# Low parts of the weight chunks by accumulating transfers issued from GpSimd, in place of a VectorE subtraction

## The chip, the core and the metric

One core of a Trainium2 chip runs the kernel. The metric is the device time of one execution in microseconds. The kernel before takes 1121.04 us (median of 2 runs, 1120.94 to 1121.14). Engines are named as in the profile: PE (TensorE; PEld is its weight load), DVE (VectorE), ACT (ScalarE), POOL (GpSimd), SP (SyncE, which issues the transfers here).

## The reference

Two transformer-like blocks run one after the other on x of 512 tokens by 1024 features, all in float32. Cut to the parts that give the large matrix products:

```python
def first_block(x, mem, ...):
    proj = rmsnorm(x, norm_g) @ w_in                  # 1024 x 4616
    y_a = mlstm_branch(...) * silu(z_a)
    y_b = pool_branch(...) * silu(z_b)
    y_c = mem_attn_branch(qc, mem, ..., w_mem_kv) * silu(z_c)
    return rmsnorm(x + concat([y_a, y_b, y_c]) @ w_out, final_norm_g)

def second_block(h, ...):
    p = h @ w_in_2 + b_in_2                           # 1024 x 7184
    y_a = spatial_gating(a_u, a_v, ...)
    y_b = gla_chunked(q, k, v, log_f) * ... * silu(r)
    h = layer_norm(ALPHA * h + (sigmoid(g_a) * y_a + sigmoid(g_b) * y_b) @ w_out_2)
    return layer_norm(ALPHA * h + square(relu(h @ w_ff1)) @ w_ff2)
```

## The kernel before, in words

**Products in parts.** Each float32 operand is split in a high part (rounded to the fp32r type of the PE) and a low part (the operand less its high part). A product is then three matmuls: high by high, high by low, low by high (`mm3`).

**Chunks.** The weights lie in HBM as 184 chunks of 128 partitions by 1024 (18 of them by 1040) float32, in the order of use; all are 512 KB, or 520 KB. `load_to` (line 631) has SP transfer chunk c to a tile `wr` (4 buffers). `split_to` (line 639) makes the high part `wh` on ACT (a Copy that rounds) and the low part `wl` on DVE (`wr` less `wh`); both have 4 buffers (`HL`, line 612). One chunk is the weights of one unit on PE, most often 8 x 3 matmuls of 512 columns (`fm`, line 718) or 16 x 3 of 256 or 260 columns (`units_tok`, line 812). `run_ahead` (line 698) names the chunks to be split while a unit runs.

**Which chunks go another way.** Chunks 0 and 1 are split piece by piece at the start (low parts on POOL). The 22 chunks 124 to 145 (`fast_ff`) go through `pair_weights` (line 731), which splits sums of them. Chunks 117 to 123 and 160 to 183 are `paged`: split into pages `pg`, in two halves. The rest (2 to 116, 146 to 159) goes through the line that the change touches, line 655.

**Order.** The program is recorded first (`Recorder`), each operation with a cost (`costs`, line 225). `schedule` (line 360) then runs a model of the engines and the buffers and writes the order of each engine's queue; transfers share one modelled wire there. Each engine works through its queue in that order, and waits in it. The order is the same in every execution.

**Side work.** Between the units the branches run in small steps: the mlstm heads and the attention early, the gated linear attention (`gla`, line 1593) in the middle, with many small POOL additions, then the layer norms. POOL also makes the residual (`resid`, line 1855).

The line at the heart of it and the helper that it calls:

```python
def split(hi, lo, src, scale=None, eng=None):
    if scale is None:
        act(hi, src, ACTF.Copy)
        tt(eng or V, lo, src, f(hi), ALU.subtract)
```

Of the kernel before, what the change touches and what calls it, by code (L numbers as in the profile page):

```python
# [11 lines left out]
ACTF = mybir.ActivationFunctionType  # L12
ALU = mybir.AluOpType
# [7 lines left out]
ISQ = 128.0 ** -0.5  # L21

SLOT = 1088

NFAST = 11

# [143 lines left out]
class Recorder:  # L170
# [54 lines left out]
    def costs(self, o):  # L225

        kw, eng = o.kw, o.eng
        out = kw["out"]
        n = out.n if isinstance(out, View) else 512
        ins = [v for k, v in kw.items() if isinstance(v, View) and k not in WRITES]  # L230
        ps = any(v.tile.psum for v in ins)
        o.port, o.table, o.tail = False, None, 60
        if eng == "PE":
            o.tail = 230
            if o.what == "transpose":
                o.cost = 112
            else:
                n = kw["rhs"].n
                slow = kw["rhs"].dt == F32
                o.cost = 2 * max(112, 0.85 * n) if slow else max(113, 0.449 * n)  # L240
        elif eng == "ACT":
            extra = sum(isinstance(kw.get(k), View) for k in ("scale", "bias"))
            o.cost = (150 if ps else 190) + 0.835 * n + 95 * extra + (206 if "accum_out" in kw else 0)
            fn = kw["func"].name if hasattr(kw["func"], "name") else str(kw["func"]).rsplit(".", 1)[-1]
            o.table = EXACT.get(fn)
        elif eng == "DVE":
            n = max(n, max((v.n for v in ins), default=0))
            ptr = any(isinstance(kw.get(k), View) for k in ("scalar", "scalar1", "scalar2"))
            big = [k for k in ("in_", "in0", "in1", "data", "mask", "data0", "data1") if isinstance(kw.get(k), View)]
            sb = [k for k in big if not kw[k].tile.psum]  # L250
            o.port = len(sb) >= 2 or (len(sb) == 1 and len(big) == 1 and o.what in ("tensor_copy", "tensor_scalar"))
            o.cost = 140 + 1.045 * n + 65 * ptr
            if o.what == "memset":
                o.cost = 50 + n
            elif o.what == "tensor_scalar" and not ps and n >= 256:
                o.cost = 140 + 0.55 * n + 65 * ptr
            elif o.what == "copy_predicated":
                o.cost = 160 + 1.1 * n
            elif o.what == "tensor_tensor_scan":
                o.cost = 1200  # L260
            elif n <= 16:
                o.cost = 165
        elif eng == "POOL":
            o.port = o.what != "memset"
            o.cost = 190 + 2.15 * n
            if o.what == "memset":
                o.cost = 515
            elif o.what == "affine_select":
                o.cost = 260 + 0.75 * n
            elif o.what == "tensor_copy":  # L270
                o.cost = 200 + 1.3 * n
        else:
            o.cost = 440
            o.tail = 2100
# [85 lines left out]
    def schedule(self, caps, prio):  # L360
        import heapq
        import numpy as np
        ops = self.ops
        n = len(ops)
        tags = list(caps)
        live = {g: np.zeros(n + 1, np.int32) for g in tags}
        for t in {t for o in ops for t in o.tiles}:
            t.left = 0
            if t.tag:
                live[t.tag][t.first] += 1  # L370
                live[t.tag][t.last + 1] -= 1
        for g in tags:
            live[g] = np.cumsum(live[g])
            assert live[g].max() <= caps[g], (g, live[g].max())
        for o in ops:
            for t in o.tiles:
                t.left += 1
        slots = {g: [0.0] * caps[g] for g in tags}
        ends = {}
        engines = ("PE", "ACT", "DVE", "POOL", "SP")  # L380
        at = dict.fromkeys(engines, 0.0)
        pend = {e: [] for e in engines}
        for o in ops:
            o.waiting, o.ready, o.start = len(o.deps), 0.0, None
        for o in ops:
            if not o.waiting:
                insort(pend[o.eng], (prio[o.i], o.i))
        head = 0
        port = 0.0
        wire = 0.0  # L390
        table = None
        best = {}
        fits = {}

        made = set()

        def room(o):

            need = {}
            for t in o.tiles:  # L400
                g = t.tag
                if not g or t in made:
                    continue
                need[g] = need.get(g, 0) + 1
                if len(slots[g]) < need[g]:
                    return False
                if t.first > head and live[g][head:t.first].max() >= caps[g]:
                    return False
            return True

        def look(e):
            got = None
            k = 0
            for _, i in pend[e]:
                o = ops[i]
                if not room(o):
                    continue
                s = max(at[e], o.ready)
                for t in o.tiles:
                    if t.tag and t not in made:  # L420
                        s = max(s, slots[t.tag][0])
                if o.port:
                    s = max(s, port)
                if got is None or s < got[0] - 1e-6:
                    got = (s, i)
                if s <= at[e] + 1e-6:
                    break
                k += 1
                if k > 60:
                    break  # L430
            return got

        done = 0
        order = []
        while done < n:
            for e in engines:
                best[e] = look(e) if pend[e] else None
            have = [(b[0], b[1], e) for e, b in best.items() if b]
            assert have, ("stuck", head, ops[head].eng, ops[head].what, {e: len(p) for e, p in pend.items()}, {g: len(s) for g, s in slots.items()})
            s, i, e = min(have)  # L440
            o = ops[i]
            pend[e].remove((prio[i], i))
            cost = o.cost
            if o.table and table not in o.table:
                table = o.table[0]
                cost += 1283
            if e == "SP":
                b = o.kw["out"]
                size = 4.0 * 128 * (b.n if isinstance(b, View) else 512)
                wire = max(wire, s + 500) + size / 250.0  # L450
                o.end = max(wire, s + cost) + 1500
            else:
                o.end = s + cost + o.tail
            o.start = s
            at[e] = s + cost
            if o.port:
                port = s + cost
            for t in o.tiles:
                if t.tag and t not in made:
                    heapq.heappop(slots[t.tag])  # L460
                    if t.first > head:
                        live[t.tag][head:t.first] += 1
                made.add(t)
            for t in o.tiles:
                t.left -= 1
                ends[t] = max(ends.get(t, 0.0), o.end)
                if not t.left and t.tag:
                    heapq.heappush(slots[t.tag], ends.pop(t))
                    if t.last >= head:
                        live[t.tag][head:t.last + 1] -= 1  # L470
            for j in o.users:
                u = ops[j]
                u.ready = max(u.ready, o.end if u.eng != e else s + cost + (0 if e != "SP" else o.end - s - cost))
                u.waiting -= 1
                if not u.waiting:
                    insort(pend[u.eng], (prio[j], j))
            while head < n and ops[head].start is not None:
                head += 1
            order.append(i)
            done += 1  # L480
        self.end = max(o.end for o in ops)
        return order
# [32 lines left out]
def tile_two_blocks(ctx, tc, wa, wb, xT, memT, vec, cst, rows, poolw, wst, wg2, out):  # L515
# [41 lines left out]
    def act(out, in_, func, **kw):  # L557
        A.activation(out=out, in_=in_, func=func, **kw)
# [44 lines left out]
    src = []  # L603
    na = nb = 0
    for kind in chunks:
# [3 lines left out]
        else:  # L609
            src.append(wb[nb])  # L610
            nb += 1
    RAW, HL = 4, 4
    raw, wsp, paged = {}, {}, set()
    FF1 = 4 + len(ORDER1) + 12 + 16 + len(ORDER2) + 8
    fast_ff = set(range(FF1 + 4, FF1 + 4 + 2 * NFAST))
# [23 lines left out]
    def split_to(i):  # L639
        while n_sp[0] <= min(i, NCH - 1):  # L640
            c = n_sp[0]
# [9 lines left out]
            else:  # L651
                o = shift.get(c, 0)
                h = rec.tile(sb, [128, SLOT], F32R, tag="wh", name=f"wh{c}", bufs=HL)[:, o:o + n]
                l = rec.tile(sb, [128, SLOT], F32R, tag="wl", name=f"wl{c}", bufs=HL)[:, o:o + n]
                split(h, l, t)
            wsp[c] = (h, l)
            n_sp[0] += 1

# [1659 lines left out]
```

## Time and profile before

| | before |
|---|---|
| median of 2 runs | 1121.04 us |
| the profiled execution, its own time | 1119.03 us |
| span of the profiled execution | 1117.3 us |
| PE busy | 1100.6 us (99%) |
| DVE busy | 771.1 us (69%) |
| ACT busy | 564.2 us (50%) |
| POOL busy | 182.7 us (16%) |
| transfers: bytes, share of 16 engines | 108.94 MB, 30.1% (queue q1) |
| mean granted clock of PE | 0.996 |

Busy times are sums over instructions of one profiled execution. The span goes from its first to its last instruction; its own time is 1.7 us more than the span. Issuing a transfer is not counted as busy. All recorded operations have one source line in the profile (L502), so groups are told apart by their tiles.

### The profile page before, as it was taken

The page shows a single profiled execution, that of the slowest core. Times are in us where ns is not written, and L with a number is a line of the kernel's source. Part 1 is how long each engine was busy: PE and PEld are TensorE (multiplying, and loading weights), DVE is VectorE, ACT ScalarE, POOL GpSimd, SP SyncE. Part 2 cuts the span into 40 slices and gives each one's busy share as a digit, 9 for nine tenths or more (in the row PEclk, how much of TensorE's full clock was granted, in tenths as well). Part 3 has the DMA queues.
Part 4 walks back from the last instruction along what each step waited for, and adds up shares of the span by engine and source line. Part 5 has one row for each costly group of instructions (what it writes and reads, how often), then busy time and mean ns, then how long its engine had stood idle before and what let it go on. Part 6 is the DMA issues. An engine that isn't in the chain of part 4 may idle for free.

```text
span 1117.3 us, 16271 instructions
## 1 busy us (share of the span) xinstructions
PE 1100.6 (99%) x6204; PEld 958.1 (86%) x6204; DVE 771.1 (69%) x1411; ACT 564.2 (50%) x964; POOL 182.7 (16%) x244
## 2 busy tenths in 40 slices
PE   7999999999999999999999999999999999999996
PEld 7888888878889999888888887899999988888885
DVE  6978888887336566667868876988898966233324
ACT  7766536444225343874655544446866666123301
POOL 5202101000012000253237550001000000000005
PEclk9999999999999999999999999999999999999998
DMA  8334322433322322232211132240133353244201
GB/s 303 114 104 148 108 76 67 151 101 108 95 94 92 101 76 76 78 94 85 84 57 57 57 98 72 89 139 1 61 111 114 114 171 96 91 132 133 75 1 76
DMA packets 33806, 108.94 MB, mean 98 GB/s; under 512 B 3888, under 2 KB 5040, under 8 KB 33728
## 3 DMA queue, kind: packets, MB, share of 16 engines
q1 hardware_dynamic: 33728, 107.90, 30.1%
q8 instruction: 49, 0.80, 0.3%
q14 instruction: 29, 0.24, 0.1%
HBM read 105.79 MB, written 2.10 MB: 97 GB/s over the span
## 4 chain that ended last, share of the span: by engine, by line
PE 96%; ACT 2%; DVE 1%; DMA 0%; issue 0%; SPq 0%; DVEq 0%
PE ps L502 96%; ACT pg L502 1%; DVE pg L502 1%; DVE wl L502 0%; DMA pg<-in_xT_dram 0%; ACT wh L502 0%; DVE sm L502 0%; SPq L502 0%; DVE sel L502 0%; DVE selc L502 0%; DVEq L502 0%
## 5 line engine op out<-in xcount | busy, mean ns | idle before, releaser
L502 PE MATMUL ps<-pg,wh 128*128 128x512 f32 (+1 forms) x1600 | 485.7, 386 | 0.0
L502 PEld LDWEIGHTS ps<-pg,wh 128*128 128x128 f32 x1600 | 294.4, 188 | 59.4 <-PE ps L502 0.7
L502 PE MATMUL ps<-pg,wl 128*128 128x512 f32 (+1 forms) x800 | 305.9, 383 | 0.0
L502 ACT ACTIVATE wh<-wr 128x1024 fp32r<-128x1024 f32 (+2 forms) x137 | 139.8, 1021 | 241.1 <-PE ps L502 209.0
L502 PE MATMUL ps<-pg,pg 128*128 128x512 f32 (+3 forms) x1264 | 236.5, 343 | 0.1
L502 ACT ACTIVATE pg<-pg 128x512 f32<-128x512 f32 (+7 forms) x328 | 174.2, 554 | 110.7 <-DVE pg L502 100.3
L502 PEld LDWEIGHTS ps<-pg,pg 128*128 128x128 f32 x1264 | 203.8, 191 | 28.8 <-ACT pg L502 0.6
L502 DVE TENSOR_TENSOR wl<-wr,wh 128x1024 fp32r<-128x1024 f32 (+1 forms) x129 | 165.0, 1282 | 76.8 <-ACT wh L502 76.3
L502 POOL TENSOR_TENSOR pg<-pg,pg 128x128 f32<-128x128 f32 (+4 forms) x113 | 109.3, 975 | 646.1 <-ACT pg L502 467.9
L502 PEld LDWEIGHTS ps<-pg,wl 128*128 128x128 f32 x800 | 150.2, 188 | 29.9
L502 PE MATMUL ps<-wh,pg 128*128 128x260 f32 (+2 forms) x800 | 168.1, 306 | 5.7 <-ACT wh L502 5.7
L502 DVE TENSOR_TENSOR pg<-pg,pg 128x512 fp32r<-128x512 f32 (+7 forms) x227 | 130.8, 603 | 23.1 <-ACT pg L502 14.9
L502 PEld LDWEIGHTS ps<-wh,pg 128*128 128x128 f32 x800 | 129.9, 190 | 12.6 <-ACT wh L502 5.7
L502 DVE TENSOR_TENSOR pg<-ps,pg 128x512 f32<-128x512 f32 (+4 forms) x128 | 80.4, 636 | 68.8 <-PE ps L502 65.3
L502 PE MATMUL ps<-wl,pg 128*128 128x260 f32 (+2 forms) x400 | 120.9, 304 | 0.1
L502 PE MATMUL ps<-pg,fh 128*128 128x256 f32 x616 | 105.4, 277 | 0.8 <-DVE pg L502 0.8
L502 PEld LDWEIGHTS ps<-pg,fh 128*128 128x128 f32 x616 | 91.8, 188 | 1.7 <-DVE pg L502 1.2
L502 DVE TENSOR_TENSOR pg<-wr,pg 128x512 fp32r<-128x512 f32 x62 | 40.7, 689 | 73.2 <-issue 45.0
L502 PE MATMUL ps<-pg,fl 128*128 128x256 f32 x308 | 81.6, 277 | 0.5 <-ACT pg L502 0.5
L502 PEld LDWEIGHTS ps<-wl,pg 128*128 128x128 f32 x400 | 75.8, 190 | 3.9 <-issue 0.5
L502 ACT ACTIVATE pg<-wr 128x512 fp32r<-128x512 f32 x62 | 35.4, 623 | 83.7 <-PE ps L502 75.2
L502 DVE SCALAR_TENSOR_TENSOR pg<-pg,pg 128x512 f32<-128x512 f32 (+4 forms) x76 | 54.7, 738 | 4.3 <-ACT pg L502 3.6
(148 smaller groups left out, 847.9 us busy)
## 6 DMA issues: line engine op xcount, KB each, us to landing
wr<-in_wa_dram SPq DMA_DIRECT2D x172, 512.0 KB, 3.6
wr<-in_wb_dram SPq DMA_DIRECT2D x10, 520.0 KB, 3.7
pg<-in_xT_dram SPq DMA_DIRECT2D x16, 256.0 KB, 4.3
pg<-in_rows_dram SPq DMA_DIRECT2D x10, 256.0 KB, 4.2
out_dram<-pg SPq DMA_DIRECT2D x8, 256.0 KB, 2.0
wr<-in_wb_dram SPq DMA_DIRECT2D x8, 130.0 KB, 4.3
pg<-in_memT_dram SPq DMA_DIRECT2D x4, 256.0 KB, 8.0
pg<-in_wst_dram SPq DMA_DIRECT2D x2, 256.0 KB, 4.5
```

Of the source, the lines that this page charges most:

```text
L502: getattr(real[o.eng], o.what)(**kw)
```

## The change

For chunks from 8 on that go through line 655, the low part is no longer a subtraction on DVE. ACT makes the high part as before, then writes the negated high part into `wl`, and a transfer issued from POOL adds the chunk, read once more from HBM, to what stands in `wl`. The planner's costs get entries for such a transfer: 1100 ns of POOL, and a wire of 170 bytes per ns where SP's transfers have 250.

```diff
+POOL_DMA = 1100
@@ costs
+        elif eng == "POOL" and o.what == "dma_start":
+            o.cost = POOL_DMA
         elif eng == "POOL":
@@ schedule
-            if e == "SP":
+            dma = o.what == "dma_start"
+            if dma:
                 b = o.kw["out"]
                 size = 4.0 * 128 * (b.n if isinstance(b, View) else 512)
-                wire = max(wire, s + 500) + size / 250.0
+                wire = max(wire, s + 500) + size / (250.0 if e == "SP" else 170.0)
                 o.end = max(wire, s + cost) + 1500
...
-                u.ready = max(u.ready, o.end if u.eng != e else s + cost + (0 if e != "SP" else o.end - s - cost))
+                u.ready = max(u.ready, o.end if u.eng != e or dma else s + cost)
@@ tile_two_blocks
-    RAW, HL = 4, 4
+    RAW, HL, ACC = 4, 4, 8
@@ split_to
-                split(h, l, t)
+                if c < ACC:
+                    split(h, l, t)
+                else:
+
+                    act(h, t, ACTF.Copy)
+                    act(l, t, ACTF.Copy, scale=-1.0)
+                    G.dma_start(out=l, in_=src[c], accum_op=ALU.add)
```

## Rows read from the trace of the kernel before

**Rows 1.** The page's part 1: busy us (share) and instructions of each engine.

```profile
PE 1100.6 (99%) x6204; PEld 958.1 (86%) x6204; DVE 771.1 (69%) x1411; ACT 564.2 (50%) x964; POOL 182.7 (16%) x244
```

**Rows 2.** Chain that ended last, in order: start us, us, what.

```profile
25.69 735.00 PE ps L502 x3965
...
1108.68 0.71 DVE sm L502
```

**Rows 3.** Windows, all instructions: busy us per engine (instructions), clock, DMA, GB/s.

```profile
core 0: us, PE busy (x) PEld busy (x) DVE busy (x) ACT busy (x) POOL busy (x), PEclk, DMA share, GB/s
0.00:25.69 25.69, 19.89 (x154) 19.69 (x154) 15.75 (x29) 19.54 (x35) 16.75 (x28) 1.00 0.89 314
...
50.00:750.00 700.00, 700.00 (x3751) 600.05 (x3750) 513.93 (x945) 350.23 (x593) 137.68 (x193) 1.00 0.29 92
...
1108.70:1117.30 8.60, 0.00 (x0) 0.00 (x0) 4.72 (x13) 0.20 (x1) 1.25 (x1) 0.65 0.26 101
```

**Rows 4.** Timeline of PE from 301 us: start us, us, operation, count.

```profile
301.06 0.39 PE L502 MATMUL ps<-pg,wl 128*128 128x512 f32 x1
301.29 0.62 PE L502 MATMUL ps<-pg,wh 128*128 128x512 f32 x2
301.74 0.39 PE L502 MATMUL ps<-pg,wl 128*128 128x512 f32 x1
```

**Rows 5.** Groups by form: busy us, mean ns | idle before, releasers.

```profile
L502 DVE TENSOR_TENSOR wl<-wr,wh 128x1024 fp32r<-128x1024 f32 x119 | 151.4, 1275 | 64.9 <-ACT wh L502 64.4
...
L502 ACT ACTIVATE wh<-wr 128x1024 fp32r<-128x1024 f32 x119 | 125.8, 1058 | 223.7 <-PE ps L502 201.7 <-issue 20.7 <-DMA wr<-in_wa_dram 1.2
...
L502 POOL TENSOR_TENSOR pg<-pg,pg 128x512 f32<-128x512 f32 x41 | 62.8, 1537 | 530.8 <-ACT pg L502 421.3 <-PE ps L502 98.6 <-DVE pg L502 9.3
```

**Rows 6.** Who waited for whom: us in total, times, longest us.

```profile
POOL pg L502 <- ACT pg L502: 525.7, 28, 300.5
ACT wh L502 <- PE ps L502: 209.0, 85, 6.1
...
SPq L502 <- DVE wl L502: 665.0, 119, 17.7
```

**Rows 7.** Windows, all instructions, first gla steps; columns as in Rows 3.

```profile
450.00:500.00 50.00, 50.00 (x220) 40.79 (x219) 31.34 (x39) 43.23 (x54) 23.31 (x39) 1.00 0.29 91
500.00:525.00 25.00, 25.00 (x119) 21.34 (x118) 20.12 (x52) 12.96 (x25) 3.91 (x7) 1.00 0.27 85
```

**Rows 8.** Page, parts 3 and 6: queue, HBM, issues to landing (KB, us).

```profile
q1 hardware_dynamic: 33728, 107.90, 30.1%
HBM read 105.79 MB, written 2.10 MB: 97 GB/s over the span
...
wr<-in_wa_dram SPq DMA_DIRECT2D x172, 512.0 KB, 3.6
```

**Rows 9.** Tile wr, SP's issues: ns min/median/max, first and last start us.

```profile
L502 SPq DMA_DIRECT2D wr<-in_wa_dram x172: 327/328/784, 16.5 to 1043.3; - x172
```

**Rows 10.** Timeline of ACT: start us, us, operation [idle before <-releaser].

```profile
317.63 1.06 ACT L502 ACTIVATE wh<-wr 128x1024 fp32r<-128x1024 f32 x1 [4.38 <-PE ps L502]
```

**Rows 11.** Timelines of DVE (chunks 8, 9) and of PE (chunk 9).

```profile
40.83 1.20 DVE L502 TENSOR_TENSOR wl<-wr,wh 128x1024 fp32r<-128x1024 f32 x1
52.33 1.20 DVE L502 TENSOR_TENSOR wl<-wr,wh 128x1024 fp32r<-128x1024 f32 x1
...
62.94 0.73 PE L502 MATMUL ps<-pg,wh 128*128 128x512 f32 x2
```

**Rows 12.** Windows, only instructions that touch wh; columns as in Rows 3.

```profile
50.00:150.00 100.00, 75.82 (x271) 47.75 (x270) 23.01 (x19) 20.45 (x20) 0.00 (x0) 1.00 0.33 104
...
250.00:500.00 250.00, 225.05 (x939) 158.83 (x939) 53.57 (x42) 45.62 (x43) 0.00 (x0) 1.00 0.30 93
500.00:650.00 150.00, 102.91 (x329) 60.98 (x328) 25.99 (x19) 21.19 (x20) 0.00 (x0) 1.00 0.21 67
```

**Rows 13.** Timelines of DVE, then POOL, near 310 us: start us, us.

```profile
310.32 2.31 DVE L502 TENSOR_TENSOR wl<-wr,wh 128x1024 fp32r<-128x1024 f32 x1
...
306.68 4.87 POOL L502 TENSOR_TENSOR pg<-pg,pg 128x512 f32<-128x512 f32 x3 [89.08 <-PE ps L502]
```

## The prediction

> **What bounds the kernel now.** I read the busy times first, then the chain of work that ended last, then windows over the stages. PE is busy 1100.6 us [rows 1] of a span of 1117.3 us. The chain shows that this is no accident of averaging: from 25.69 us on it runs through PE's own instructions, 735.00 us of them in one piece, and leaves PE for good only at 1108.68 us [rows 2]. The 16.7 us in which PE is idle lie 25.69 - 19.89 = 5.8 us in the head, 8.6 us in the tail, and the remaining 2.3 us between; from 50 to 750 us, where most of the changed chunks are split, PE is busy 700.00 of 700.00 us at a granted clock of 1.00 [rows 3]. Three 512-column matmuls take 301.74 - 301.06 = 0.68 us there, so a unit of 24 takes 8 x 0.68 = 5.44 us [rows 4]. That pace is what everything else has to keep up with. DVE, from which the change takes work, is nowhere in that piece of the chain. So the question is not what DVE gains, but whether the new way to make a low part is late for PE.
>
> **The change, part by part.** *How many.* Of 184 chunks, 176 have numbers from 8 on; less 22 fast and 31 paged ones leaves 123 (8 of them with 1040 columns, priced like the rest).
>
> *Removed from DVE:* 123 x 1.275 = 157 us [rows 5]; DVE falls from 771 to about 614 us. The gain in time is nothing: PE does not wait for DVE there.
>
> *Added to ACT:* 123 x 1.058 = 130 us, taking the negated copy at the price of the high part, which has the same form [rows 5]; ACT rises from 564 to 694 us (62%). The cover is ACT's waiting: it waits 209.0 us for PE to give back a `wh` buffer [rows 6]. Where the cover is thin: from 450 to 500 us ACT is busy 43.23 us [rows 7], and 50 / 5.44 = 9 chunks x 1.06 make that 52.7 us, 2.7 us more than there is. The next 25 us have 12 us free [rows 7], so the surplus moves there. If half of it reaches PE, it costs 1.3 us. I take that; the ends are 0 and 2.7 us.
>
> *Moved on SP's queue:* a load into `wr` waits for the last reader of the old chunk, now the subtraction (665.0 us of waits, which cost nothing, [rows 6]), after the change ACT's second copy. That ends 1.06 us after the high part instead of 1.28: loads start when they did. Each still lands 3.6 us after its issue [rows 8].
>
> *Added to POOL's queue:* 123 issues. The trace has no transfer issued from POOL. Bounds: 0.33 us, what an issue takes on SP [rows 9], and 1.5 us, POOL's own dearest common addition [rows 5]. I take 1.1, nearer to an instruction of POOL's own; 123 x 1.1 = 135 us brings POOL from 183 to 318 us (28%). An issue waits in the queue for ACT's negated copy, and POOL's additions for the gla heads and the residual stand behind it.
>
> *Added to the DMA engines:* 123 transfers that add. No row shows one. A plain chunk: queue q1 moved 107.90 MB in 30.1% of 1117.3 us = 336 us of all 16 engines, 3.12 us per MB, so 1.63 us for 512 KB [rows 8]. Low bound: the same, 1.63 us. High bound: reading HBM, reading `wl` and writing `wl` as three passes, 4.9 us. I take two, for the two operands that are read: 3.27 us. The traffic of SP's loads stays beside it.
> The Trainium skill, Collectives: The Full Stack, section "The bandwidth ceiling: the fold count and why AG ≠ RS ≠ AR", says that an adding step is slower for its two source reads and not for the add, and so runs at about half the rate of a copy; the estimate by that page is the same 2 x 1.63 us. No row here shows it.
>
> **Does it keep up?** *Latency.* ACT refills a `wh` buffer the moment PE frees one: 4.38 us of waiting and 1.06 us of work make the 5.44 us of a unit [rows 10]. With four buffers, that chunk is used three units later, after 3 x 5.44 = 16.3 us. The new chain is 1.06 + 1.06 on ACT, 1.1 on POOL, and the landing: 3.6 - 1.63 = 2.0 us beyond the data, plus 3.27, so 5.3 us. Together 8.5 us; 7.8 us are spare. With three passes it is 10.1 us, still in time. Tightest at the start: the subtraction of chunk 9 begins at 52.33 us, so its high part is done then, and PE begins that chunk at 62.94 us [rows 11]; 52.33 + 1.06 + 1.1 + 5.3 = 59.8 us, at the dear end 61.4. In time.
>
> *Throughput.* From 50 to 150 us 20.45 / 1.058 = 19.3 chunks are split while the DMA engines are 33% busy, so (100 - 33) / 19.3 = 3.47 us are free for each adding transfer; from 250 to 500 us 45.62 / 1.058 = 43.1 chunks at 30%, (250 - 75) / 43.1 = 4.06 us [rows 12]. My 3.27 fits both, with 0.2 us to spare in the first. This is the narrow place of the whole argument.
>
> *Hold-ups between DVE and POOL.* At 310.32 us a subtraction takes 2.31 us, beside a POOL addition that runs until 311.55 us [rows 13], where others take 1.20 [rows 11]. One such collision costs 1.1 us and a wait for the whole of it 2.3 us; for a transfer both are under the 7.8 us spare, so the sum stays, but they count in rival B.
> The Trainium skill, SBUF — State Buffer, section "SBUF: two separate sides", speaks against this change: GpSimd cannot write the descriptors of its transfers while DVE runs in its two-port mode. By its example, 620 ns becoming 3100, each transfer would come 2.5 us later, an estimate that is under the spare as well. No row here shows a transfer that is blocked.
>
> **Sum.** Profiled execution 1119.0 + 1.3 (ACT, 450 to 500 us) + 0 for DVE + 0 for the transfers = 1120.3 us. The median of the runs, 1121.04, stands 2.0 us above the profiled execution, so 1122.3 us; I say 1122.
>
> **The rivals.**
> *A. The adding transfers bound the kernel.* It decides from 3.47 us per transfer on; with 4.06 the loss is (4.06 - 3.47) x 19.3 = 11 us, still within 2%. At three passes (4.9 us): (4.9 - 3.47) x 19.3 = 28 us from 50 to 150 us, (4.9 - 4.06) x 43.1 = 36 us from 250 to 500 us, and for chunks 146 to 159 14 x (1.63 + 4.9 - 5.44) = 15 us: 79 us, 1201 us. For it: nothing shows the price, and the first stretch has hardly any room. Against: buffers for three chunks smooth it. Chance 0.10 for up to 22 us (about 1132), 0.14 for more.
> *B. POOL's queue holds transfers back.* In the gla stage POOL's small additions wait for ACT and DVE, in order, and a transfer behind one waits too. POOL waited 525.7 us for ACT in 28 waits [rows 6], though with nothing urgent behind it. It decides once a hold exceeds the 7.8 us spare. Price: if each of the 9 chunks of 450 to 500 us and of the 21.19 / 1.058 = 20 chunks of 500 to 650 us [rows 12] is 1 us late, 29 us, 1151 us. Against: POOL is busy only 23.31 of 50 us there [rows 7], and the order is written with the transfers in it. Chance 0.07.
> *C. Faster by over 2%.* All of PE's idle time is 16.7 us, 1.5%, and the change takes no matmul away. If DVE's relief took half of the head's 5.8 us, the time would be 1119. Over 2%: 0.02.
> *As summed:* 0.67.
>
> **How the numbers follow.** Within 2% (1098.6 to 1143.5 us, about what a measurement can tell from no change): 0.67 + 0.10 = 0.77. Slower: 0.14 + 0.07 = 0.21. Faster: 0.02. The likeliest case alone spans 1118 to 1127. The range for 8 in 10 goes from 1114, 1122 less the 5.8 us of the head and the 2.3 us between, to 1160, which takes in the mild form of A and B and leaves out A's dear form.
>
> **What would show it.** Right: PE busy near 1100 us, idle near 17 us; `wl` written by DVE for the first few chunks only, DVE near 614 us, ACT near 694 us; HBM read up from 105.79 MB [rows 8] by 123 x 0.52 = 64 to 170 MB; a second queue whose packets take about 123 x 3.27 = 402 us of 16 engines (36%). A shows as PE waiting for a transfer into `wl` between 50 and 150 and from 250 to 500 us, with a DMA share near 1. B shows as that wait between 450 and 650 us, with issues long after ACT's copy. The prediction is wrong if the new queue takes over 4.2 us per transfer, or if `wl` lands over 16 us after PE freed its buffer.

## The result, and the profile after

| | before | after |
|---|---|---|
| median | 1121.04 us (2 runs) | 1132.88 us (2 runs, 1132.02 and 1133.74) |
| ratio | | 1.0106, 95% interval 1.0062 to 1.0149 |
| the profiled execution, its own time | 1119.03 us | 1133.74 us |
| span | 1117.3 us | 1132.1 us |
| mean granted clock of PE | 0.996 | 0.992 |

The changed kernel is 11.8 us, 1.06%, slower. That is within 2%, and the interval leaves no room for "no difference". The time lies inside the range of the prediction, 1114 to 1160 us, but not inside the 1118 to 1127 us of its likeliest case.

The page of after, part 1 (busy us, share of the span, instructions of each engine), part 3 (queue: packets, MB, share of 16 engines) and part 6 (KB each, median us from issue to landing). On POOL the issues are counted here as busy.

```profile
PE 1106.1 (98%) x6204; PEld 960.2 (85%) x6204; DVE 625.6 (55%) x1288; ACT 675.8 (60%) x1085; POOL 267.2 (24%) x367
...
q0 software_dynamic: 17712, 64.56, 32.3%
q1 hardware_dynamic: 33728, 107.90, 30.9%
...
HBM read 170.34 MB, written 2.10 MB: 152 GB/s over the span
...
wl<-in_wa_dram POOLq DMA_DIRECT2D x115, 512.0 KB, 7.4
```

The work moved as described: DVE fell from 771.1 us [rows 1] to 625.6, ACT rose from 564.2 to 675.8, HBM reads from 105.79 MB [rows 8] to 170.34, and a second queue q0 stands beside SP's q1. One adding transfer took 32.3% of 1132.1 us / 123 = 2.97 us of all 16 engines, an SP load 30.9% of 1132.1 / 107.90 x 0.524 = 1.70 us.

PE is busy 5.5 us longer with the same 6204 matmuls, and idle 1132.1 - 1106.1 = 26.0 us in place of 16.7. So there are two kinds of loss: 9.3 us of idleness, and matmuls that ran slower. The chain of after says where the idleness is (start us, us, what):

```profile
24.60 54.87 PE ps L506 x293
...
84.26 9.38 DMA wl<-in_wa_dram
...
93.68 384.95 PE ps L506 x2152
...
478.66 307.42 PE ps L506 x1589
...
907.57 8.53 DMA wl<-in_wa_dram
...
916.14 207.54 PE ps L506 x906
```

Before, PE held the chain from 25.69 us for 735 us without a break [rows 2]. Now it breaks twice for a transfer into `wl`, once near 90 us and once near 910 us, and the landings there took 9.38 and 8.53 us. Between these places, from 94 to 786 us, PE holds it again almost alone. The waits of PE name the same two (waiter, awaited: us in total, times, longest):

```profile
PE ps L506 <- ACT wh L506: 8.8, 2, 5.9
PE ps L506 <- DMA wl<-in_wa_dram: 5.0, 2, 2.5
```

PE waits for a transfer in just two places, 5.0 us in all; of the 8.8 us for ACT's high part, 5.9 are in the head (5.7 us before), and 2.9, at the second of these places, are new. Most of the rest of the 9.3 us is in short waits for ACT between 786 and 892 us (3.7 us in 8 waits; before, 2.1 us in 4 waits for ACT and DVE). The kernel without transfers below has them too (2.9 us in 6) and loses no time.

To see the loss with the clock in it, I counted matmul columns in both traces and took, for the same share of the columns done, the difference in time (worked out from the PE records; records missing from either trace make it good to some tenths of a microsecond):

```
share of the columns   before (us)   after minus before (us)
0.050                     64.4             +0.2
0.100                    118.4             +4.8
0.400                    446.2             +4.6
0.450                    498.8             +6.5
0.625                    698.8             +6.5
0.800                    900.1             +7.2
0.825                    926.2            +15.0
1.000                   1108.6            +15.0
```

Nearly the whole loss of this pair of executions lies in three steps: 4.6 us near 90, 1.9 us between 446 and 499, 7.8 us near 910. (From 740 to 905 us the two kernels do their work in different orders and the figure moves between 4.4 and 7.2.) The windows at these steps and over the long stretches (columns as in Rows 3):

```profile
50.00:150.00 100.00, 97.47 (x512) 81.21 (x511) 62.27 (x109) 73.26 (x128) 27.12 (x39) 0.98 0.88 200
...
90.00:100.00 10.00, 7.47 (x27) 5.47 (x27) 2.24 (x4) 3.98 (x10) 1.47 (x3) 0.83 1.03 249
250.00:500.00 250.00, 249.97 (x1500) 221.59 (x1500) 90.61 (x179) 153.14 (x200) 59.05 (x72) 0.99 0.79 177
500.00:650.00 150.00, 150.00 (x721) 128.14 (x720) 98.83 (x295) 103.00 (x191) 83.51 (x146) 1.00 0.72 155
...
910.00:920.00 10.00, 4.70 (x11) 3.39 (x12) 2.50 (x4) 7.71 (x11) 2.59 (x3) 0.67 1.04 266
915.00:920.00 5.00, 3.86 (x9) 3.10 (x10) 2.50 (x4) 2.74 (x5) 0.86 (x1) 0.50 1.08 275
```

From 250 to 650 us, where two rivals were expected to bite, PE has practically no gap (249.97 of 250.00 and 150.00 of 150.00 us), with the DMA engines at 0.72 to 0.79. At 90 and 910 us their share is over 1 (the times of all packets, added up, exceed the time of 16 engines), PE stands still, and the granted clock is 0.83 and 0.67 in the 10 us with the wait. Behind the second wait it is 0.50, from 915 to 920 us: PE runs there at the lower of its two levels (1.2 and 2.4 GHz).

**The place at 90 us.** POOL's timeline (start us, us, operation [idle before <-releaser]):

```profile
82.83 1.48 POOL L506 TENSOR_TENSOR pg<-pg,pg 128x256 f32<-128x256 f32 x2 [0.90 <-DVE pg L506]
84.26 0.87 POOL L506 DMA_DIRECT2D wl<-in_wa_dram  x1
85.75 0.85 POOL L506 DMA_DIRECT2D wl<-in_wa_dram  x1 [0.63 <-ACT wl L506]
88.77 0.86 POOL L506 DMA_DIRECT2D wl<-in_wa_dram  x1 [2.16 <-ACT wl L506]
90.97 0.86 POOL L506 DMA_DIRECT2D wl<-in_wa_dram  x1 [1.34 <-ACT pg L506]
```

and ACT's and PE's for the chunk that is late, chunk 15:

```profile
80.34 1.05 ACT L506 ACTIVATE wh<-wr 128x1024 fp32r<-128x1024 f32 x1
81.30 1.04 ACT L506 ACTIVATE wl<-wr 128x1024 fp32r<-128x1024 f32 x1
...
80.56 0.28 PE L506 MATMUL ps<-pg,wl 128*128 128x256 f32 x1
...
80.90 0.28 PE L506 MATMUL ps<-pg,wl 128*128 128x256 f32 x1
...
90.01 0.67 PE L506 MATMUL ps<-pg,wh 128*128 128x512 f32 x2
90.52 0.63 PE L506 MATMUL ps<-pg,selc 128*4 128x512 f32 x2
93.68 0.50 PE L506 MATMUL ps<-pg,wl 128*128 128x512 f32 x1 [2.53 <-DMA wl<-in_wa_dram]
```

The units before it have 256 columns: a triple takes 80.90 - 80.56 = 0.34 us, a unit 8 x 0.34 = 2.72 us, half of the 5.44 us of [rows 4]. So the four buffers come free at twice the pace and are needed again after half the time. Chunk 15's high part begins 9.7 us before PE opens the unit; its negated copy is done at 82.34 us; POOL is then held by its own additions, which waited for DVE, and issues at 84.26. Four transfers are issued within 7 us, this one first, and their landings take 9.38, 11.06, 11.93 and 12.9 us. PE waits 2.53 us for the first; the other 2.1 us of the step are put down to the lower clock behind the wait. POOL's hold is 84.26 - 82.34 = 1.9 us long: had the transfer been issued at 82.34 us and landed as slowly, PE would have waited some 0.6 us (an estimate).

**The place at 910 us.** ACT, POOL and PE of after, where the fast pairs hand over to chunks 146 and on:

```profile
905.28 1.04 ACT L506 ACTIVATE wh<-wr 128x1024 fp32r<-128x1024 f32 x1
906.22 1.04 ACT L506 ACTIVATE wl<-wr 128x1024 fp32r<-128x1024 f32 x1
...
911.78 1.04 ACT L506 ACTIVATE wh<-wr 128x1024 fp32r<-128x1024 f32 x1
...
907.57 0.88 POOL L506 DMA_DIRECT2D wl<-in_wa_dram  x1 [115.09 <-ACT wl L506]
...
908.89 1.09 PE L506 MATMUL ps<-pg,wh 128*128 128x512 f32 x4
912.88 0.84 PE L506 MATMUL ps<-pg,wh 128*128 128x512 f32 x2 [2.89 <-ACT wh L506]
916.14 0.80 PE L506 MATMUL ps<-pg,wl 128*128 128x512 f32 x1 [2.42 <-DMA wl<-in_wa_dram]
```

The fast pairs hold all four pairs of buffers in `wh` and `wl`, so chunk 146's high part begins only 908.89 - 905.28 = 3.6 us before PE starts on it. Before, the same hand-over looked like this on ACT and on PE:

```profile
897.40 1.06 ACT L502 ACTIVATE wh<-wr 128x1024 fp32r<-128x1024 f32 x1
...
901.74 0.63 PE L502 MATMUL ps<-pg,wh 128*128 128x512 f32 x2
902.21 0.39 PE L502 MATMUL ps<-pg,wl 128*128 128x512 f32 x1
```

A lead of 4.3 us was enough for a copy and a subtraction of 2.3 us together [rows 5], and PE had no gap. The new way takes 907.57 + 8.53 - 905.28 = 10.8 us from the start of the high part to the landing. PE's queue has the first high-part matmuls of chunks 146, 147 and 148 there, two of each, before the first one with chunk 146's low part. So PE waits twice: 2.89 us for the high part of chunk 148, which ACT makes only at 911.78 us, behind a negated copy and other work, and then 2.42 us for the landing. Together with some 2.5 us of the lower clock that is the step. The first of these waits is ended by ACT and not by a transfer: in this order PE would have waited it also if the landing had been in time.

The DMA engines had little room at this place before either, when SP's loads went alone (window of before, columns as in Rows 3):

```profile
900.00:905.00 5.00, 5.00 (x32) 4.43 (x32) 4.30 (x6) 3.80 (x7) 0.00 (x0) 1.00 0.95 372
```

### The profile page after: what moved, and what is told of

It reads as the page before. It is cut to its first block, busy times and chain, and to the rows that moved or that the text cites. A ratio compares the mean times of both kernels' runs of the same rounds, so it can differ in the third digit from the quotient of the medians.

```text
span 1132.1 us, 16517 instructions
## 1 busy us (share of the span) xinstructions
PE 1106.1 (98%) x6204; PEld 960.2 (85%) x6204; DVE 625.6 (55%) x1288; ACT 675.8 (60%) x1085; POOL 267.2 (24%) x367
## 3 DMA queue, kind: packets, MB, share of 16 engines
q0 software_dynamic: 17712, 64.56, 32.3%
q1 hardware_dynamic: 33728, 107.90, 30.9%
HBM read 170.34 MB, written 2.10 MB: 152 GB/s over the span
## 4 chain that ended last, share of the span: by engine, by line
PE 85%; issue 10%; DMA 2%; DVE 1%; ACT 1%; SPq 0%; DVEq 0%; POOLq 0%
PE ps L506 85%; DMA wl<-in_wa_dram 2%; DVE pg L506 1%; ACT pg L506 1%; ACT wh L506 0%; DMA pg<-in_xT_dram 0%; DVE sm L506 0%; DVE wl L506 0%; SPq L506 0%; DVE sel L506 0%; DVE selc L506 0%; DVEq L506 0%; POOLq L506 0%
## 5 line engine op out<-in xcount | busy, mean ns | idle before, releaser
L506 POOL DMA_DIRECT2D wl<-in_wa_dram x115 | 100.0, 870 | 534.9 <-ACT wl L506 490.7
L506 ACT ACTIVATE pg<-pg 128x512 f32<-128x512 f32 (+8 forms) x328 | 173.9, 553 | 59.6 <-DVE pg L506 50.2
L506 DVE TENSOR_TENSOR pg<-pg,pg 128x512 f32<-128x512 f32 (+6 forms) x227 | 137.9, 632 | 93.9 <-ACT pg L506 75.0
L506 POOL TENSOR_TENSOR pg<-pg,pg 128x128 f32<-128x128 f32 (+4 forms) x113 | 103.4, 934 | 232.7 <-ACT pg L506 216.7
L506 ACT ACTIVATE wl<-wr 128x1024 fp32r<-128x1024 f32 (+1 forms) x123 | 128.9, 1048 | 32.1 <-PE ps L506 32.1
L506 PE MATMUL ps<-pg,fl 128*128 128x256 f32 x308 | 85.1, 278 | 1.9 <-ACT pg L506 1.9
L506 ACT ACTIVATE pg<-wr 128x512 fp32r<-128x512 f32 x62 | 35.1, 622 | 75.8 <-PE ps L506 69.7
L506 PEld LDWEIGHTS ps<-wl,pg 128*128 128x128 f32 x400 | 75.8, 190 | 3.7 <-issue 0.5
```

Source lines behind the costliest of these rows:

```text
L506: getattr(real[o.eng], o.what)(**kw)
```

## The experiments

Each ratio is to executions of the kernel before that were taken beside the run. Their median is 1120.51 us for the first three runs and the one with transfers that do not add, and 1121.09 us for the others.

The theory after the result: **the new way is too long for two places where the lead is short** (latency, in bursts of transfers), and harmless elsewhere. Rivals: the adding itself (its price on the DMA engines), ACT's 130 us, the order written with too short a landing in mind, and plain lack of DMA throughput. The first four kernels ran on one chip (before there: 1120.51 us, 22 runs), the other four on another (before there: 1121.09 us, 14 runs).

### DVE keeps chunks 8 to 18

```diff
-                if c < ACC:
+                if c < 19:
```

> Undoes the change for chunks 8 to 18 only (low part by DVE's subtraction again). Theory 'bursts' (time is lost only where several chunks have to be split within a few us: after the 256-column km units near 90 us and after the fast pairs near 908 us): the wait for wl at 93.68 us (2.53 us) and the fall of the clock behind it go, 4.6 us of the 15.0 us are given back, about 1128 us. Rival 'the added traffic and the added ACT work cost a little everywhere': 11 of 123 chunks undone give 11/123 x 12 = 1 us back, about 1132 us.

Measured: 1131.17 us (1129.94 to 1131.87, 4 runs), ratio 1.0096 [1.0075, 1.0116]. By the column count, this kernel's trace stands at +1.5 us behind the first place, in place of +4.8, and ends at +10.5 in place of +15.0. The window there (columns as in Rows 3) shows no gap and the full clock:

```profile
90.00:100.00 10.00, 10.00 (x48) 8.13 (x48) 6.96 (x12) 5.62 (x13) 2.49 (x3) 1.00 1.02 320
```

So the first step goes away in the trace. Two smaller waits for a transfer into `wl` stand behind it, which the kernel after does not have: 0.51 us at 116.42 us and 1.09 us at 475.00. The median gave back only 1.7 us of the 4.6, and lies between the expectations: as a measurement of the time this run does not decide.

### DVE keeps chunks 146 to 149

```diff
-                if c < ACC:
+                if c < ACC or 146 <= c < 150:
```

> Undoes the change for chunks 146 to 149 only, the first four after the fast pairs. Theory 'bursts': the two waits near 912 and 916 us (2.89 and 2.42 us) and the granted clock of 0.67 from 910 to 920 us go, about 8 us are given back, about 1125 us. Rival 'a little everywhere': 4/123 x 12 = 0.4 us back, about 1132.5 us.

Measured: 1124.85 us (1123.2 to 1126.51, 9 runs), ratio 1.0035 [1.0021, 1.005]: four chunks give back 8.0 of the 11.8 us, as expected. The window shows PE without a gap:

```profile
905.00:920.00 15.00, 15.00 (x86) 13.07 (x84) 10.79 (x15) 12.60 (x19) 0.88 (x1) 1.00 0.72 228
```

### Both

```diff
-                if c < ACC:
+                if c < 19 or 146 <= c < 150:
```

> Both: chunks 8 to 18 and 146 to 149 by DVE, the other 108 by accumulating transfers. Theory 'bursts': 4.6 + 8 = 12.6 us of the 15.0 back, within 3 us of the kernel before, 1119 to 1124 us. Rival 'a little everywhere': 15/123 x 12 = 1.5 us back, about 1131 us.

Measured: 1123.34 us (1122.75 to 1126.73, 12 runs), ratio 1.0028 [1.0017, 1.0038]. With 108 of 123 transfers left, three quarters of the loss are gone; 2.8 us stay. In its trace PE waits twice for a transfer into `wl`, 0.35 us at 117.00 us and here (timeline of PE):

```profile
483.63 0.50 PE L506 MATMUL ps<-pg,wl 128*128 128x512 f32 x1 [1.01 <-DMA wl<-in_wa_dram]
```

The traced execution, 1126.73 us, is the slowest of the twelve, so where the 2.8 us of the median lie is not shown. Even so repaired, the change is not faster than the kernel before: no gain from DVE's relief is to be seen.

### Only chunks 146 to 149 by transfer

```diff
-                if c < ACC:
+                if not 146 <= c < 150:
```

> The change for chunks 146 to 149 alone; the other 119 keep DVE's subtraction. Theory 'bursts': these four transfers alone cost what their removal gave back (1132.9 - 1124.9 = 8 us): about 1128.5 us, with PE waiting for wh and wl behind the fast pairs and the clock falling there. Rival 'a little everywhere': 4/123 of 12 us, about 1121 us.

Measured: 1128.78 us (1124.95 to 1129.63, 5 runs), ratio 1.0059 [1.0037, 1.0081]. The four transfers cost 7.7 us by themselves. PE's timeline at that place:

```profile
906.95 0.73 PE L506 MATMUL ps<-pg,wh 128*128 128x512 f32 x2 [2.12 <-ACT wh L506]
910.40 0.79 PE L506 MATMUL ps<-pg,wl 128*128 128x512 f32 x1 [2.72 <-DMA wl<-in_wa_dram]
```

and the landing of the four (KB each, median us):

```profile
wl<-in_wa_dram POOLq DMA_DIRECT2D x4, 512.0 KB, 10.5
```

The queue moves 2.10 MB in the whole execution, so no lack of throughput over the span can be meant. It is the lead of that place against a landing that is long there: PE waits for the first of the four, which took 8.64 us, with the DMA share at 1.03 from 905 to 910 us.

### Transfers that do not add

```diff
-                    G.dma_start(out=l, in_=src[c], accum_op=ALU.add)
+                    G.dma_start(out=l, in_=src[c])
```

> The transfers from POOL are plain ones that overwrite wl with the chunk, in place of adding to it; so the low part is not the low part (it leaves out the subtraction), and only the price of the transfer is looked at. If the 2.97 us of 16 engines per transfer and the 7.4 us to landing are the price of adding (two operands read): the POOL queue's share falls from 32.3% to about 123 x 1.65 / 1125 = 18%, and landing to about 5.5 us. If they are the price of a transfer issued from POOL: both stay, near 32% and 7.4 us.

Measured: 1128.86 us in one run. The page of this kernel, queues and landing:

```profile
q0 software_dynamic: 17712, 64.56, 16.7%
...
wl<-in_wa_dram POOLq DMA_DIRECT2D x115, 512.0 KB, 4.5
```

A plain transfer takes 16.7% of 1127.2 us / 123 = 1.53 us of 16 engines, the adding one 2.97 us, 1.94 times as much, and lands in 4.5 us in place of 7.4. With it the first step is gone (+0.8 us before and behind it), but the place at 910 us still costs 7.0 us (+3.1 before it, +10.1 behind). PE's timeline there:

```profile
908.79 0.99 PE L506 MATMUL ps<-pg,wh 128*128 128x512 f32 x2 [2.89 <-ACT wh L506]
910.65 0.80 PE L506 MATMUL ps<-pg,wl 128*128 128x512 f32 x1 [0.86 <-DMA wl<-in_wa_dram]
```

The wait for ACT's third high part is the same 2.89 us. Even a plain transfer, with a lead of 3.6 us and a landing of 7.12 us at this place, comes 0.86 us later still. So without the adding the first step does not come, and of the second the adding is only a part. This rests on one execution.

### No transfer at all

```diff
-                    G.dma_start(out=l, in_=src[c], accum_op=ALU.add)
```

> ACT's negated copy stays, the transfer is left out (so wl holds the negated high part and the low part is left out). If ACT's added 130 us are hidden, as the prediction said: nothing is lost at 90 us, and near 908 us at most the 2 to 3 us for which the second copy delays the first chunks: 1121 to 1125 us. If ACT is what makes the kernel slower: about 1131 us, with PE waiting for ACT near 90 and 480 us.

Measured: 1120.97 us (10 runs), ratio 0.9997 [0.9983, 1.001], with ACT busy 676.5 us. So ACT's second copies, as work, cost nothing, and DVE's relief gains nothing: the 11.8 us come with the transfers. They come in two ways, which this run does not part. The planner also writes another order when there are no transfers: PE takes chunk 146's unit in one piece there and has no wait. The 2.89 us for ACT's high part therefore go with the order that the planner writes around the transfers.

### The order written for later landings

```diff
-                o.end = max(wire, s + cost) + 1500
+                o.end = max(wire, s + cost) + (1500 if e == "SP" else 4500)
```

> All 123 transfers, but the planner is told that a transfer from POOL lands 3 us later (4500 ns behind its wire in place of 1500), near the 7.4 us that were measured. If the stall near 90 us comes of an order written for transfers that land sooner: the order puts ACT's copies and the issue ahead of other work, the 2.5 us wait goes, about 1128 us. If it comes of the burst itself (four chunks in 11 us, buffers that come free 8 us ahead and not 16): it stays, 1131 to 1134 us. The stall near 908 us stays in both.

Measured: 1131.52 us (1130.41 to 1133.82, 4 runs), ratio 1.0093 [1.0072, 1.0113]: inside the expectation for "not the order". The trace is more mixed. At the first place the step shrinks from 4.6 to 1.9 us, with a wait of 0.69 us for ACT's high part at 108.61 in place of 2.53 for the transfer at 93.68, and a new wait of 1.02 us for a transfer stands at 482.38. At the last place the step stays 7.9 us, now with two waits for ACT's high part, 2.89 and 1.16 us. So this order helps a little at the first place and not at the second, and the median stays. An order in which PE's queue does not open chunk 148 ahead of chunk 146's low part was not tried.

### SP's loads twice

```diff
             SP.dma_start(out=t, in_=src[c])
+            if 8 <= c < 117:
+                SP.dma_start(out=t, in_=src[c])
```

> All 123 transfers, and SP loads chunks 8 to 116 twice into the same buffer, so that each chunk costs 1.70 + 1.70 + 2.97 = 6.37 us of all 16 engines where a unit takes 5.44 us. If the kernel after stands close under the bound of the DMA engines (rival A): (6.37 - 5.17) x 19.3 = 23 us from 50 to 150 us and 43.1 x 6.37 - 250 = 25 us from 250 to 500 us come on top, about 1180 us, with PE waiting for transfers at a DMA share near 1. If there is more room than that sum says: under 1145 us.

Measured: 1211.13 us (1205.13 and 1217.14), ratio 1.0807 [1.0739, 1.0874], more than either theory gave. SP's queue moves 165.12 MB in place of 107.90. The window from 250 to 500 us (columns as in Rows 3):

```profile
250.00:500.00 250.00, 228.71 (x1364) 201.57 (x1363) 85.02 (x177) 116.32 (x159) 41.49 (x43) 0.96 0.84 231
```

The largest waits of PE, and one of ACT:

```profile
PE ps L506 <- ACT wh L506: 24.6, 12, 6.2
PE ps L506 <- DMA wl<-in_wa_dram: 23.1, 10, 5.1
...
ACT wh L506 <- DMA wr<-in_wa_dram: 27.0, 5, 11.7
```

With 1.70 us more per chunk on the engines, PE loses time all along: +22.2 us by 118 us, +33.0 by 256, +75.8 by 499. For the first stretch the sum of rival A gives (2.97 + 1.70 - 3.47) x 19.3 = 23 us and the trace 22; for 250 to 500 us it gives (2.97 + 1.70 - 4.06) x 43.1 = 26 us and the trace 43, with the DMA engines only 84% busy. The share near 1 that was expected did not come either from 50 to 150 us, where it is 0.86. So it is not throughput alone: the second load also makes the high part later, and ACT waited 27.0 us for loads into `wr`. How the two share the loss was not separated. That the kernel after has little room left on the DMA engines fits this run and is not proved by it.

## Why the prediction was right or wrong

**The bound.** Right. PE bounds both kernels, and DVE's relief is worth nothing: DVE ended at 625.6 us (614 predicted), and without the transfers, with DVE relieved, the time is that of the kernel before (ratio 0.9997).

**ACT.** Right, 675.8 us against 694: a copy added 111.6 / 123 = 0.91 us of busy time, set down at 1.06. The 1.3 us set down for 450 to 500 us did not come: from 450 to 650 us no PE wait for `wl` or `wh` is to be found in the trace of after, and the run without transfers costs nothing. What was missed is the place at 910 us, where ACT's queue makes PE wait 2.89 us in the order written around the transfers.

**POOL's issues.** 0.87 us each, taken at 1.1, between bounds of 0.33 and 1.5. The rule of the Trainium skill in SBUF — State Buffer, section "SBUF: two separate sides", is that GpSimd cannot write its descriptors while DVE is in its two-port mode. No run here shows it: the 123 issues took between 0.83 and 1.18 us, but whether DVE was ever in that mode, and whether a landing holds such a wait, is not known.

**The price on the DMA engines.** Right: 2.97 us, 3.27 predicted, bounds 1.63 and 4.9. The ratio to a plain transfer, 1.94, agrees with the half rate that the Trainium skill gives for the adding steps of a collective in Collectives: The Full Stack, section "The bandwidth ceiling: the fold count and why AG ≠ RS ≠ AR".

**Throughput.** Right on the whole. The DMA share was 0.88 from 50 to 150 us and 0.79 from 250 to 500 us; 33 + 19.3 x 2.97 = 90 and 30% + 43.1 x 2.97 / 250 = 81% were to be expected from the measured price. The doubled loads cost about what a limit of 3.47 us in the first stretch would make of them, 22 us for 23, but with a DMA share of 0.86; they do not prove the limit. Rival A showed only as bursts of 10 us, with a share over 1 near 90 and 910 us and long landings in them, and not as a stretch that is bound.

**Latency: the step that failed.** The prediction said that a buffer's next chunk is used "three units later, after 3 x 5.44 = 16.3 us", that the chain takes 8.5 us, that "7.8 us are spare", and that chunk 9 was the tightest. Three terms were wrong:
- *The lead.* 16.3 us holds where units have 512 columns and the ring of four buffers turns freely. After units of 256 columns it is 3 x 2.72 = 8.2 us by the same count (chunk 15 had 9.7), and behind the fast pairs, which hold all four buffers, it is 3.6 us. The prediction mentioned neither, though both stood in the trace of before: the hand-over at 897.40 to 901.74 us could have been read there, and 3.6 or 4.3 us against 8.5 says at once that PE will wait 4 to 5 us (5.3 were measured). It looked for the tightest place at the start only.
- *The landing.* 5.3 us were estimated for one transfer among moderate traffic; the median was 7.4 us, from 5.2 to 12.9, and it was 9 to 13 us where four were under way within 7 us. A plain one from POOL already lands after 4.5 us, 0.9 later than SP's 3.6 [rows 8]; the adding brought 2.9 more where 1.6 was set down.
- *POOL's hold.* It was put at nothing, because 7.8 us seemed to be spare. At the first place it was 1.9 us. There the lead alone would have done: 9.7 us against the 8.5 of the sum. The hold and a landing of 9.38 us in place of 5.3 made it late.

The criterion offered for being wrong, "lands over 16 us after PE freed its buffer", inherited the mistake: at the two places the low part landed 13.3 and 10.8 us after ACT had begun the high part in the freed buffer, and PE waited all the same.

**What a wait costs.** The prediction priced waits by their length. Each of the two places cost about 2 us more: the rows show granted clocks of 0.83 and 0.67 in the 10 us with the wait, and 2.1 of the 4.6 us, and 2.5 of the 7.8, remain when the waits are taken off.

**Rival B.** Between 450 and 650 us, where it was priced, no wait for a transfer stands in the trace of after. Its mechanism did show at the first place, where POOL's queue held chunk 15's issue for 1.9 us (82.34 to 84.26).

**The sum.** The sum came to +1.3 us, against +11.8. The two places give 4.6 + 7.8 = 12.4 us in the profiled execution. By the medians the second place is worth 7.7 to 8.0 us, shown both by taking its four transfers away and by adding them alone; the first is worth only 1.5 to 1.7 us (1132.88 - 1131.17, and 1124.85 - 1123.34), and 2.8 us stay with both undone, whose place is not shown. The third step, 1.9 us between 446 and 499 us, need not be the change's: the kernel without transfers has a like one in its trace (+1.6 us, granted clock 0.83 from 455 to 465 us) and yet the median of the kernel before. The profiled execution of before was one without it, which may be a part of why it stands 2.0 us under the median.

That the time fell into the range was luck in part: the range was that wide for rivals A and B, and 1132.9 us is near the 1132 of A's mild form, but the cause was a short lead met by long landings at two places, which no rival named.

## What to carry to other kernels

Before trading a short on-chip operation for a transfer, list the places where a buffer is filled least long before its use (behind short units, and behind a stage that holds the whole ring), and compare the new latency with the smallest lead, not with the lead of the steady state. Take the landing time from a moment with several transfers under way, and add to each expected wait of TensorE the time that it will run at the lower clock behind it. Look also at what the planned order puts ahead of the late buffer: a wait can be for the work that was moved forward. Relieving DVE, which is not on the chain, bought nothing here, so this trade could only lose. If one like it is made for another reason, leave the short-lead chunks to the old way: here four chunks of 123 held two thirds of the loss.

## What the runs showed of the hardware that was not expected

- An adding transfer of 512 KB into on-chip memory took 1.94 times the engine time of a plain one (2.97 and 1.53 us of 16 engines), landed 2.9 us later (7.4 and 4.5 us median), and its issue kept POOL longer too (0.87 and 0.54 us).
- Four of them issued within some 8 us, beside SP's loads, landed in 8.5 to 12.9 us each, with the DMA share at 1.03 to 1.05 over 10 us, also where the rest of the execution had no such transfer (10.5 us median of four).
- In seven of the ten traces, also that of the kernel without transfers, the granted clock over 455 to 465 us is between 0.66 and 0.85 with PE busy without a gap. In those of before and of the kernel with DVE to chunk 18 it is 1.00 (the tenth, with the doubled loads, has other work there). The work of PE just ahead was the same in before and after, twelve matmuls of 16 rows in 3.03 us, at 451.48 us in before. PE's timeline of after:

```profile
456.07 3.03 PE L506 MATMUL ps<-pg,pg 16*128 16x512 f32 x12
```

and the windows of after behind it:

```profile
455.00:460.00 5.00, 5.00 (x21) 3.55 (x20) 3.39 (x5) 3.24 (x5) 0.77 (x1) 0.94 0.87 183
460.00:465.00 5.00, 5.00 (x17) 3.92 (x17) 0.75 (x1) 4.95 (x8) 0.00 (x0) 0.72 0.16 32
```

The clock is 0.94 and then 0.72 with PE busy 5.00 of 5.00 us; in before it is 1.00 in both windows. What decides whether it falls is open.
